# A hybrid decoder layer: load order and splits at its start, softplus steps, and one low part moved to VectorE

## The chip, the cores and the metric

The kernel runs on one core of a Trainium2 chip. The metric is the device time of one execution in microseconds (us), the median over runs. TensorE (PE) multiplies matrices into PSUM; VectorE (DVE), ScalarE (ACT) and GpSimd (POOL) do the elementwise work; SyncE (SP) issues the DMA transfers. Each engine works off its own queue in order.

## The reference

One decoder layer on 1040 tokens (16 learned meta tokens ahead of 1024), width 1024, all in float32. The part that matters here is its start:

```python
xn = rms_norm(h, mix_pre_g)                  # pre-norm
proj = xn @ w_in                             # z | x, B, C | dt | q | k | v
...
xbc = silu(causal_dwconv(xbc, conv_w, conv_b))   # 4 taps
dt = softplus(dt_raw + dt_bias)
Adt = dt * A
...                                          # SSD scan over chunks of 128, decays from cumsum(Adt)
y = rms_norm((y_diag + y_off + xs * d_skip) * silu(z), norm_g)
```

Behind it come a stick-breaking attention on q, k, v, an output projection, and a feed-forward block with a convolution of 3 taps. The change touches none of these.

## The kernel before

**Precision.** A matmul in float32 is made of three in a faster format: each operand is split into a high part (`hi`, a copy that rounds, by ScalarE) and a low part (`lo` = value minus high part, by VectorE or GpSimd), and the products hi·hi, hi·lo and lo·hi are added in PSUM. So every weight tile must be loaded (raw), split, and only then used. Names: `wr_` or `r` is a raw tile, `whi`/`wh_`/`ah` a high part, `wlo`/`wl_`/`al` a low part.

**Order.** Everything here is written inside regions of a manual schedule: within a region each engine executes its instructions in the order in which the program emits them. There are two such regions one behind the other, the *head* (lines 323 to 611) and *order* (from line 613). How instructions of the one fall among those of the other on an engine is left to the scheduler. SyncE's queue belongs to the head region too.

**The head.** It loads nine token tiles (`load_x`, tile 0 being the 16 meta tokens), the pre-norm's weights broadcast to all partitions (`gpre`, 512 KB), and weights. For tile i, `square(i)` on ScalarE sums the squares, `root(i)` makes the reciprocal root in two small steps on GpSimd (lines 169 and 170), `norm(i)` multiplies on VectorE (line 369), and `turn_x(i)` transposes on PE (line 383); ScalarE copies the high parts and two raw sums (lines 393 to 396), and VectorE subtracts for the low parts (line 402). Between them stand the products that can start early: dt (`dt_steps`, `pj_dt`), B (`pj_B`) and C (`pj_C`) of group 0, each in four parts over the tokens (`chains`, one part run at a time). `split_hi` and `split_lo` make B's and C's high part on ScalarE and low part on VectorE. At the head's end the sums of tokens that a Strassen scheme needs are split (`t1` to `t3`: line 254 on ScalarE, 255 on VectorE).

**The order region.** Column blocks of the projection are made in pairs (`Duo`): x, z, x, z, B and C, and so on. A pair takes seven products (Strassen's scheme in Winograd's form), each of 24 matmuls into one of the banks A, X or Y. Products 1 and 2 are copied out by ScalarE, the others added to an earlier result by VectorE (line 320), and a bank that goes on accumulating waits for that add. Beside the products of a pair run, in slots behind each product:

- the preparation of the next pair's weights: `split_22` (one quarter, 128x512: high part `ah` on ScalarE, line 277, low part `al` on GpSimd, line 278), `sums` (four additions of 128x512 on GpSimd, lines 285 to 288), `split_3`, `split_1`, `split_4` (whole tiles; low parts on GpSimd, line 182);
- what is left to do for the pair before (convolution taps on VectorE, lines 505 and 508; silu on ScalarE; transposes to token order);
- the steps of dt (`dt_acts`).

The first pair (`i == 0`, x) takes its products in the order 1, 5, 2, 6, 7, 3, 4. Behind product 1 it emits `d0.split_4()`, then `split_22` of the next pair (z), then slot 0, in which are taps 0 and 1 of B's convolution and dt's loads; slot 1, behind product 5, has B's taps 2 and 3. Product 7 goes on in the bank of product 6, behind its add.

dt's steps: `turn_dt` (dt to token order by small matmuls, line 649), `soft_a` and `soft_b` (softplus as a series on VectorE, with one exponential on ScalarE), three `decay` steps (each a matmul on PE, lines 682 and 683, and exponentials), the last with the stores.

Of the kernel before, what the change touches and what calls it, by code (L numbers as in the profile page):

```python
# [9 lines left out]
F32 = mybir.dt.float32  # L10
# [3 lines left out]
ALU = mybir.AluOpType  # L14
# [52 lines left out]
def tile_layer(ctx: ExitStack, tc: tile.TileContext, x, meta, rows, parts,  # L67
# [190 lines left out]
    class Duo:  # L258
# [11 lines left out]
        def split_1(self):  # L270
            self.w["a11"], self.w["a12"] = split_w(self.r[0], f"1{self.nm}")

        def split_22(self):
            h, l = (weight_rows(sa.tile([P, 5 * P], F32R, tag=f"a22{e}", name=f"a{e}{self.nm}", bufs=2), 4, OFF22)
                    for e in "hl")
            raw = self.r[1][:, HI4]
            nc.scalar.activation(h, raw, AF.Copy)
            nc.gpsimd.tensor_tensor(l, raw, h.bitcast(F32), op=ALU.subtract)
            self.w["a22"] = h, l

        def sums(self):
# [42 lines left out]
    with tc.tile_pool(name="pre", bufs=3, side="right") as pre:  # L324
# [3 lines left out]
        def load_x(i):  # L328
            xts.append(pre.tile([P, D], F32, tag="xt", name=f"xt{i}", bufs=8))
            nc.sync.dma_start(out=xts[i][:spans[i][1]], in_=meta if i == 0 else x[(i - 1) * P:i * P, :])  # L330

        def raw_of(name, src):
            raw = wp.tile([P, KB, P], F32, tag="wraw", name=f"wr_{name}")
            nc.sync.dma_start(out=raw, in_=src)
            return raw

        load_x(0)
        load_x(1)
        raws = {"B0": raw_of("B0", w_xbc[8])}
        gpre = row_bcast(pre, 0, D, "gpre")  # L340
        load_x(2)
        load_x(3)
        raw_dt = pre.tile([P, KB, 16], F32, tag="wdt", name="wr_dt", bufs=1)
        nc.sync.dma_start(out=raw_dt, in_=w_dt)
# [9 lines left out]
        def square(i):  # L354
            if i <= NT:
                nr = spans[i][1]
                junk = pre.tile([P, D], BF16, tag="junk", name=f"junk{i}", bufs=1)
                sums[i] = pre.tile([P, 1], F32, tag="ss", name=f"ss{i}")
                nc.scalar.activation(junk[:nr], xts[i][:nr], AF.Square, scale=D ** -0.5, accum_out=sums[i][:nr])
# [5 lines left out]
        def norm(i):  # L365
            if i <= NT:
                nr = spans[i][1]
                norms[i] = pre.tile([P, D], F32, tag="xn", name=f"xn{i}", bufs=2)
                nc.vector.scalar_tensor_tensor(norms[i][:nr], xts[i][:nr], roots[i][:nr], gpre[:nr],
                                               op0=ALU.mult, op1=ALU.mult)  # L370
# [3 lines left out]
        def turn_x(i):  # L374
            t0, nr = spans[i]
            tps = []
            for hf in range(2):
                tp = (psum_tp, psum_z, psum_sd)[(2 * i + hf) % 3](f"xtp{i}_{hf}")
                if (2 * i + hf) % 3:
                    tp = tp.rearrange("p (a b) -> p a b", b=P)  # L380
                for b in range(4):
                    k = 4 * hf + b
                    nc.tensor.transpose(tp[:, b, :nr], norms[i][:nr, k * P:(k + 1) * P], ident[:nr, :nr])
                tps.append(tp)
            cuts = [(t0, t0 + nr)] if t0 >= TH or t0 + nr <= TH else [(t0, TH), (TH, t0 + nr)]
            sub, copy = nc.vector.tensor_tensor, nc.scalar.activation
            for a, e in cuts:
                half = a // TH
                c = (slice(None), slice(None), slice(a - half * TH, e - half * TH))
                p0, p1 = (tp[:, :, a - t0:e - t0] for tp in tps)  # L390
                pairs = [(p0, xo[f"b1{1 + half}"]), (p1, xo[f"b2{1 + half}"])]
                for src, (h, _) in pairs:
                    copy(h[c], src, AF.Copy)
                copy((t1r, t3r)[half][c], p0, AF.Copy)
                if half == 0:
                    copy(t4r[c], p1, AF.Copy)
                for r, o in ((TH - 8, 0), (L - 8, 8)):
                    if a <= r < e:
                        for hf in range(2):
                            copy(xtail[:, 4 * hf:4 * hf + 4, o:o + 8], tps[hf][:, :, r - t0:r - t0 + 8], AF.Copy)  # L400
                for src, (h, l) in pairs:
                    sub(l[c], src, h[c].bitcast(F32), op=ALU.subtract)
                    if half and src is p0:
                        sub(t1r[c], p0, t1r[c], op=ALU.subtract)
                if half:
                    sub(t2r[c], p1, t1r[c], op=ALU.subtract)
                    late.append(lambda c=c: nc.vector.tensor_tensor(t4r[c], t4r[c], t2r[c], op=ALU.subtract))
                    sub(t3r[c], p1, t3r[c], op=ALU.subtract)
# [3 lines left out]
        def split_hi(name):  # L412
            hi = wp.tile([P, KB, P], F32R, tag="whi", name=f"wh_{name}", bufs=WB)
            lo = wp.tile([P, KB, P], F32R, tag="wlo", name=f"wl_{name}", bufs=WB)
            nc.scalar.activation(hi, raws[name], AF.Copy)
            ws[name] = hi, lo

        def split_lo(name):
            nc.vector.tensor_tensor(ws[name][1], raws[name], ws[name][0].bitcast(F32), op=ALU.subtract)
# [3 lines left out]
            root(i)  # L423
        norm(0)
        norm(1)
        split_hi("B0")
        split_lo("B0")
        square(2)
        root(2)
        norm(2)  # L430
        turn_x(0)
        square(3)
        root(3)
        norm(3)
# [190 lines left out]
    def dt_acts():  # L625
# [30 lines left out]
        def soft_a():  # L656
            dtx = box["dtx"]
            e, s, s2 = box["e"], box["s"], box["s2"] = [t3(n) for n in ("e1", "s1", "s2")]
            nc.vector.scalar_tensor_tensor(e, dtx, -1.0, dtx, op0=ALU.mult, op1=ALU.min)
            nc.scalar.activation(e, e, AF.Exp)  # L660
            nc.vector.tensor_scalar(s, e, 2.0, None, op0=ALU.add)
            nc.vector.reciprocal(s, s)
            nc.vector.tensor_tensor(s, s, e, op=ALU.mult)
            nc.vector.tensor_tensor(s2, s, s, op=ALU.mult)
# [13 lines left out]
        def decay(k):  # L678
            lhs = (tri, low, ones)[k]
            pz, adt, dst = psum_mm(f"pz{k}"), box["s2"], dtk[:, 2 + k]  # L680
            w0 = P if k == 2 else NM
            mm(pz[:w0, 0:16], lhs[:NM, :w0], adt[:NM, 0, :], start=True, stop=True)
            mm(pz[:, 16:NA], lhs, adt[:, 1:, :], start=True, stop=True)
            nc.scalar.activation(dst[:w0, 0, :], pz[:w0, 0:16], AF.Exp)
            nc.scalar.activation(dst[:, 1:, :], pz[:, 16:NA].rearrange("p (a b) -> p a b", b=16), AF.Exp)
            if k == 0:
                nc.vector.tensor_copy(dtk[:NM, 1, 0, :], pz[:NM, 0:16])
                nc.vector.tensor_copy(dtk[:, 1, 1:, :], pz[:, 16:NA].rearrange("p (a b) -> p a b", b=16))
# [15 lines left out]
        def store():  # L704
            nc.sync.dma_start(out=dtkd, in_=dtk)

        return [[loads], [turn_dt], [soft_a], [soft_b], [lambda: decay(0)], [lambda: decay(1)],
                [lambda: decay(2), store, turn_acs]]

    v_stack = ExitStack()  # L710
# [29 lines left out]
    def merged(*lists):  # L740
        return [sum(parts_, []) for parts_ in zip(*lists)]
# [5 lines left out]
    for i, q in enumerate(duos):  # L747
        n = duos[i + 1] if i + 1 < len(duos) else None
        if i + 2 < len(duos):
            duos[i + 2].load()  # L750
        for j, m in enumerate((1, 5, 2, 6, 7, 3, 4) if i == 0 else (1, 6, 5, 7, 2, 3, 4)):
            q.product(m)
            if i == 0:
                if m == 1:
                    d0.split_4()
                elif m == 6:
                    split_t(t4l.bitcast(F32), xo["t4"], nc.vector)
            if n is not None:
                if m == 1:
                    n.split_22()  # L760
                elif m == 6:
                    n.sums()
                elif m == 7:
                    n.split_3()
                elif m == 2:
                    n.split_1()
                elif m == 3:
                    n.split_4()
            elif m in (7, 2):
                v_split(1, int(m == 2))  # L770
            for act in slots[j]:
                act()
        extra = slots[7:]
        slots = q.done(q)
        for k, acts_ in enumerate(extra):
            slots[k] = acts_ + slots[k]
        if i == 1:
            slots = merged(slots, [[], dts[2], [], dts[3], [], [], []]) + [dts[4], dts[5], dts[6]]
        if i == n_early:
            t_stack.close()  # L780
            vl = v_stack.enter_context(tc.tile_pool(name="vl", bufs=1, side="left"))
            fetch_v(1, 0, vl)
        if i + 2 == len(duos):
            fetch_v(0, 0, None)
# [1711 lines left out]
```

## Time and profile before

| | |
|---|---|
| time of three runs | 1655.59 to 1659.79 us, median 1657.96 |
| the profiled execution, its time | 1657.8 us |
| its span on the core | 1655.8 us |
| granted clock of TensorE, mean of the span | 0.997 |
| instructions | 28995 |
| busy: PE, VectorE, GpSimd, ScalarE | 98%, 66%, 47%, 45% of the span |
| traffic in DRAM | 148 GB/s over the span |
| idle time of PE in the first 300 us, by the releaser | 12.1 us for the pre-norm, 2.9 us for others |

The span runs from the first to the last instruction of the execution; its time has some 2 us around it. A row of a timeline gives the start and the duration in us, the engine, the line of the kernel, the operation, out<-in with shapes, and in brackets how long the engine had stood idle before and what released it. Waits for several semaphores are put down to one of them. In the rows of the windows the busy time of PE, of its weight loads, VectorE, ScalarE and GpSimd follow one another, with the count of instructions, then the granted clock, the share of the DMA engines and GB/s.

### The profile page before, as it was taken

To read this page: it belongs to the slowest core of one execution; us is meant where nothing else is said; L and a number is where in the kernel's file an instruction comes from. 1 tells how busy PE (TensorE), PEld (TensorE's weight loads), DVE (VectorE), ACT (ScalarE), POOL (GpSimd) and SP (SyncE) were. 2 spreads that over 40 slices of the span, in tenths; PEclk is the share of its full clock that TensorE was granted. 3 is DMA by queue.
4 is the path that set the end of the run, shared out by engine and by line. 5 is a ranking of instruction groups with operands and counts; after the bars stand their busy time and mean duration, and the time that the engine had idled before them with its cause. 6 is when DMAs were issued, how large, how long until landed. Compare 5 with 4: busy or idle time off the path is not lost.

```text
span 1655.8 us, 28995 instructions
## 1 busy us (share of the span) xinstructions
PE 1626.7 (98%) x11508; PEld 1434.1 (87%) x11508; DVE 1087.5 (66%) x1248; ACT 748.1 (45%) x1100; POOL 782.1 (47%) x579
## 2 busy tenths in 40 slices
PE   7999999999999999999999999999999999999998
PEld 6999999978877888888877889999999999888886
DVE  6975744344367599999840677765666556658877
ACT  7454344332234367766741445433333333344544
POOL 2876877520457463454421113777777677200001
PEclk9999999999999999999999999999999999999999
DMA  4544335334588776545254542222333322495345
GB/s 173 185 154 133 104 121 194 135 138 145 148 236 266 212 235 207 155 123 154 60 193 151 165 161 90 96 96 96 98 107 113 108 98 83 142 332 175 96 119 180
DMA packets 164518, 247.39 MB, mean 149 GB/s; under 512 B 18487, under 2 KB 99495, under 8 KB 162702
## 3 DMA queue, kind: packets, MB, share of 16 engines
q1 hardware_dynamic: 163806, 244.48, 45.8%
q8 instruction: 91, 1.49, 0.4%
q10 hardware_dynamic: 576, 1.05, 0.2%
q14 instruction: 45, 0.37, 0.1%
HBM read 161.99 MB, written 83.46 MB: 148 GB/s over the span
## 4 chain that ended last, share of the span: by engine, by line
PE 89%; DVE 5%; issue 2%; POOL 2%; DMA 2%; ACT 1%; POOLq 0%; DVEq 0%; SPq 0%; ACTq 0%
PE fX L1900 10%; PE mo L1504 10%; PE dnA L2312 7%; PE fY L1900 7%; PE fA L1900 7%; PE dnB L2312 5%; PE av L1352 3%; PE tw L1332 3%; PE z L1308 3%; PE pj_q L218 3%; DVE kp L1314 2%; PE pj_k L218 2%; PE dXz L308 2%; PE dXqk L308 2%; PE dXx L308 2%
## 5 line engine op out<-in xcount | busy, mean ns | idle before, releaser
L1314 DVE TENSOR_TENSOR_SCAN kp<-kp,hold 128x396 f32<-128x396 f32 (+5 forms) x224 | 211.2, 1014 | 20.2 <-ACT kp L1309 18.4
L182 POOL TENSOR_TENSOR wlo<-wr,whi 128x1024 fp32r<-128x1024 f32 x43 | 99.3, 2318 | 40.8 <-ACT whi L181 40.8
L2349 POOL TENSOR_TENSOR fms<-fms 128x1 f32<-128x1 f32 x8 | 2.3, 288 | 222.0 <-DMA ar<-fda 185.9
L181 ACT ACTIVATE whi<-wr 128x1024 fp32r<-128x1024 f32 x43 | 45.7, 1063 | 112.2 <-PE fX L1900 76.2
L1972 DVE SCALAR_TENSOR_TENSOR ga<-gr,pp,ga 128x1024 f32<-128x1024 f32 x44 | 69.4, 1577 | 34.1 <-ACT ga L1965 33.3
L2234 ACT ACTIVATE dh<-ar 128x512 fp32r<-128x512 f32 x77 | 48.6, 631 | 94.1 <-PE dnB L2312 44.7
L2235 DVE TENSOR_TENSOR dl<-ar,dh 128x512 fp32r<-128x512 f32 x77 | 53.2, 691 | 47.1 <-ACT dh L2234 47.1
L1309 ACT ACTIVATE kp<-z 128x788 f32<-128x788 f32 (+4 forms) x96 | 72.7, 832 | 16.6 <-PE z L1308 12.4
L1337 ACT ACTIVATE th<-tw 128x1024 f32<-128x1024 f32 (+2 forms) x96 | 70.8, 813 | 15.6 <-PE tw L1332 15.6
L1352 PE MATMUL av<-th,v 128*64 128x128 f32 x1152 | 70.0, 275 | 2.0 <-POOL tmsa L985 0.9
L1332 PE MATMUL tw<-ident,kp 128*128 128x128 f32 x576 | 70.0, 276 | 0.8 <-ACT st L935 0.5
L1332 PEld LDWEIGHTS tw<-ident,kp 128*128 128x128 f32 x576 | 62.4, 141 | 8.0 <-issue 6.5
L1352 PEld LDWEIGHTS av<-th,v 128*64 128x64 f32 x1152 | 62.3, 137 | 8.0 <-issue 3.9
L2312 PE MATMUL dnA<-dl,dh 128*128 128x512 f32 x176 | 68.5, 389 | 0.0
L2312 PE MATMUL dnA<-dh 128*128 128x512 f32 x176 | 68.5, 389 | 0.0
L2312 PE MATMUL dnA<-dh,dl 128*128 128x512 f32 x176 | 68.5, 389 | 0.0
L1286 POOL TENSOR_SCALAR cb<-kp 128x32 f32<-128x32 f32 x64 | 42.9, 678 | 50.5 <-DVE kp L1314 46.9
L2033 POOL TENSOR_TENSOR al<-wr,ah 128x512 fp32r<-128x512 f32 x20 | 28.6, 1430 | 77.6 <-ACT ah L2032 77.5
L1308 PE MATMUL z<-k,q 64*128 64x396 f32 (+9 forms) x672 | 62.3, 329 | 1.0 <-DVE st L941 1.0
L1308 PEld LDWEIGHTS z<-k,q 64*128 64x128 f32 x672 | 53.1, 185 | 10.8 <-ACT th L1337 4.2
L2312 PE MATMUL dnB<-dh 128*128 128x512 f32 x132 | 51.3, 389 | 0.0
L2312 PE MATMUL dnB<-dh,dl 128*128 128x512 f32 x132 | 51.3, 389 | 0.0
(987 smaller groups left out, 6026.4 us busy)
## 6 DMA issues: line engine op xcount, KB each, us to landing
wr<-in_w_up SPq DMA_DIRECT2D x44, 512.0 KB
fds<-ga SPq DMA_DIRECT2D x44, 256.0 KB
b<-in_w_down SPq DMA_DIRECT2D x44, 256.0 KB
ar<-fds SPq DMA_DIRECT2D x44, 256.0 KB
fda<-ga SPq DMA_DIRECT2D x33, 256.0 KB
ar<-fda SPq DMA_DIRECT2D x33, 256.0 KB
k<-qkd SPq DMA_DIRECT2D x8, 1040.0 KB
q<-qkd SPq DMA_DIRECT2D x64, 128.0 KB
```

The source lines that it names most:

```text
L182: nc.gpsimd.tensor_tensor(l, raw, h.bitcast(F32), op=ALU.subtract)
L218: mm(acc[:, :CQ - s], a[:, k, :], b[:, k % 4, c + s:c + CQ], start=(k == 0 and j == 0), stop=(k == KB - 1 and j == 2))
L308: mm(acc[:, c, :CQ], u[:, k, :], v[:, k, c * CQ:(c + 1) * CQ], start=first and k == 0 and j == 0, stop=k == 3 and j == 2, skip_group_check ...
L1308: mm(z[:, j, a - lo:e - lo], u[h, :], r[h, a - bases[x]:e - bases[x]], start=s_ == 0, stop=s_ == 2)
L1309: nc.scalar.activation(kp[:, :, lo:top], z[:, :, :top - lo], AF.Sigmoid, scale=-QSCALE)
L1314: nc.vector.tensor_tensor_scan(part, part, hold[:, L - last + a:L - last + e][:, ::-1], 1.0 if e == last else kp[:, j, e:e + 1], op0=ALU.m ...
L1332: nc.tensor.transpose(tw[:, j, b, :], kp[:, j, c0:c0 + P], ident)
L1337: copied[0] = nc.scalar.activation(th[:, :, :nb, :], tw[:, :, :nb, :], AF.Copy, scale=-1.0, bias=1.0).ins
L1352: mm(av[halves[j], 1 - x, :], v[:, kb, halves[j]], th[:, j, b, :], start=kb == 0, stop=kb == i)
L1504: recent[0] = mm(acc, u[:, k, :], v[:, cs], start=(k == 0 and j == 0), stop=(k == 7 and j == 2))
L1900: mm(acc[:, c, :nn], u[:, k, :], v[:, k, c0:c0 + nn], start=first and k == 0 and j == 0, stop=k == 3 and j == 2, skip_group_check=not first)
L2312: mm(banks[BANK[n], t], u[:, 0, c], v[:, 1, :], start=(n in (1, 2, 5) and p == 0 and i == 0), stop=(p == NPR - 1 and i == 2), skip_group_c ...
```

## The change

It has three parts.

1. At the head, the loads of the pre-norm's weights and of token tile 2 are issued ahead of B's weights. Square, root and norm of tile 2 come ahead of B's split; its high part comes ahead of the turn of tile 0, its low part behind it.
2. dt's softplus step `soft_a` ends with the exponential; what followed there is a step of its own, `soft_m`. During the third pair `soft_a` stays behind the second product, `soft_m` comes behind the third, `soft_b` behind the fifth instead of the fourth. The decays stay where they are.
3. `split_22` takes the engine of its subtraction as an argument. For the first pair, that is for the weights of the first z pair, it is VectorE; for all others it stays GpSimd.

```diff
-        def split_22(self):
+        def split_22(self, eng=nc.gpsimd):
...
-            nc.gpsimd.tensor_tensor(l, raw, h.bitcast(F32), op=ALU.subtract)
+            eng.tensor_tensor(l, raw, h.bitcast(F32), op=ALU.subtract)
...
         load_x(0)
         load_x(1)
-        raws = {"B0": raw_of("B0", w_xbc[8])}
         gpre = row_bcast(pre, 0, D, "gpre")
         load_x(2)
+        raws = {"B0": raw_of("B0", w_xbc[8])}
         load_x(3)
...
         norm(0)
         norm(1)
-        split_hi("B0")
-        split_lo("B0")
         square(2)
         root(2)
         norm(2)
+        split_hi("B0")
         turn_x(0)
+        split_lo("B0")
         square(3)
         root(3)
         norm(3)
...
             nc.vector.scalar_tensor_tensor(e, dtx, -1.0, dtx, op0=ALU.mult, op1=ALU.min)
             nc.scalar.activation(e, e, AF.Exp)
+
+        def soft_m():
+            e, s, s2 = box["e"], box["s"], box["s2"]
             nc.vector.tensor_scalar(s, e, 2.0, None, op0=ALU.add)
...
-        return [[loads], [turn_dt], [soft_a], [soft_b], [lambda: decay(0)], [lambda: decay(1)],
+        return [[loads], [turn_dt], [soft_a], [soft_m], [soft_b], [lambda: decay(0)], [lambda: decay(1)],
                 [lambda: decay(2), store, turn_acs]]
...
                 if m == 1:
-                    n.split_22()
+                    n.split_22(nc.gpsimd if i else nc.vector)
...
         if i == 1:
-            slots = merged(slots, [[], dts[2], [], dts[3], [], [], []]) + [dts[4], dts[5], dts[6]]
+            slots = merged(slots, [[], dts[2], dts[3], [], dts[4], [], []]) + [dts[5], dts[6], dts[7]]
```

## The prediction

> **What bounds the kernel now.** I read the page first, then the waits of TensorE (PE) in the first 300 us, then the timelines of the single engines. PE fills the span, and all that the change touches lies in the first 130 us, so the question is only which waits of PE there go or come. In the waits the columns are total, number, longest.
>
> ```profile
> span 1655.8 us, 28995 instructions
> PE 89%; DVE 5%; issue 2%; POOL 2%; DMA 2%; ACT 1%; POOLq 0%; DVEq 0%; SPq 0%; ACTq 0%
> ...
> PE xtp L383 <- DVE xn L369: 12.1, 5, 10.2
> PE dXz L308 <- POOL wlo4z L182: 1.0, 1, 1.0
> ```
>
> Beside small ones of 0.6 and 0.3 us and the one at 69.23 (quoted below), these are all of PE's waits up to 300 us. PE stands until 10.2 us and in pieces until 16.8, and once at 85.5. A microsecond saved before either place moves all that follows, since PE is busy nearly without a break behind it; a microsecond that PE doesn't wait for is worth nothing. The sum is made against the profiled execution: 1657.8 us, of which 1655.8 are span. The median of the three runs, 1657.96, is 0.2 above it, less than their scatter (4.2).
>
> **Part 1, the order at the start.** Timelines, start and duration first, idle time before and its releaser in brackets:
>
> ```profile
> 7.18 1.06 ACT L415 ACTIVATE wh_B<-wr_B 128x1024 fp32r<-128x1024 f32 x1
> 10.04 1.06 ACT L359 ACTIVATE junk<-xt 128x1024 bf16<-128x1024 f32 x1 [1.80 <-DMA xt<-in_x]
> ...
> 16.61 0.62 ACT L393 ACTIVATE b21h<-xtp 128x512 fp32r<-128x512 f32 x1
> ...
> 21.60 0.38 ACT L249 ACTIVATE sq<-pj_dt 32x260 f32<-32x260 f32 x1 [0.41 <-PE pj_dt L247]
> 8.83 2.47 DVE L369 SCALAR_TENSOR_TENSOR xn<-xt,rs_pre,gpre 16x1024 f32<-16x1024 f32 x2 [6.71 <-DMA gpre<-in_rows]
> 11.23 1.20 DVE L419 TENSOR_TENSOR wl_B<-wr_B,wh_B 128x1024 fp32r<-128x1024 f32 x1
> 13.21 1.28 DVE L369 SCALAR_TENSOR_TENSOR xn<-xt,rs_pre,gpre 128x1024 f32<-128x1024 f32 x1 [0.78 <-POOL rs_pre L170]
> 15.26 1.49 DVE L369 SCALAR_TENSOR_TENSOR xn<-xt,rs_pre,gpre 128x1024 f32<-128x1024 f32 x1 [0.50 <-POOL rs_pre L170]
> ...
> 23.13 1.22 DVE L419 TENSOR_TENSOR wl_C<-wr_C,wh_C 128x1024 fp32r<-128x1024 f32 x1
> 7.22 0.23 POOL L169 TENSOR_SCALAR ms_pre<-ss 128x1 f32<-128x1 f32 x1 [2.07 <-ACT junk L359]
> 11.28 1.24 POOL L169 TENSOR_SCALAR ms_pre<-ss 128x1 f32<-128x1 f32 x1 [3.17 <-ACT junk L359]
> ...
> 13.26 1.31 POOL L169 TENSOR_SCALAR ms_pre<-ss 128x1 f32<-128x1 f32 x1
> 16.80 1.97 PE L383 MATMUL xtp<-ident,xn 128*128 128x128 f32 x8 [0.29 <-DVE xn L369]
> 18.42 1.22 PE L247 MATMUL pj_dt<-b11h,wh_dt 128*32 128x260 f32 x4
> ...
> 25.39 0.28 PE L218 MATMUL pj_C<-b11h,wl_C 128*128 128x260 f32 x1
> ```
>
> The transfers land one behind the other: B's weights by 7.2 (ScalarE starts on them then, unwaited), the norm's weights at 8.8, token tile 2 at 10.0. All three are 512 KB, so in the new order I put the same three landings: norm's weights about 7.4, tile 2 about 8.7, B's weights about 10.0 (an estimate; the total ahead of 10.0 is unchanged). On SyncE's queue B's load is passed by these two and passes none. Behind them the load of x's first weights waits for B's low part, which frees its buffer (12.4, now about 13.5); what is queued behind it has time, its weights being read past 40.
>
> ScalarE: square 2 moves from 10.04 to 8.7, and B's high part takes its place at 10.04 with the same 1.06. So ScalarE reaches tile 0's copies at 11.1 as before, and as it has hardly an idle moment from 10.04 until its wait before 21.60 it gains next to nothing. VectorE: norms 0 and 1 at 7.4 to 9.9. GpSimd: root 2 at 9.9 and not at 12.5. Its first step takes 0.23 alone, but 1.24 and 1.31 where B's low part (11.23) or norm 2 (13.21) runs on VectorE: it waits until that ends. Norm 2 then runs at 10.8 to 12.0, B's low part at 12.2 to 13.5, root 3 behind that at 13.5 to 14.3, norm 3 at 14.3 to 15.6. Before, norm 3 ended at 16.75; 1.2 earlier. PE's transposes of tile 3 and the first product of dt (18.42) follow it directly: 17.2. The next to be late is ScalarE's copy of tile 2 (ends 17.2, in time), then C's low part, which stays at 24.3 less about 0.2, while PE wants it at 25.4 less 1.2: just in time. I take **-1.1**; bounds 0 (ScalarE, which gains nothing, takes over) and -1.6 (the wait for root 3 vanishes too). B's low part, now 1.2 to 2 later, is covered: PE's first use is past 20. From norm 6 on the VectorE chain follows PE, so the gain is carried to 42 us and beyond.
>
> **Part 2, the softplus.** It adds and drops no instruction.
>
> ```profile
> 115.79 1.17 DVE L661 TENSOR_SCALAR s<-e 128x144 f32<-128x144 f32 x1 [2.75 <-ACT e L660]
> ...
> 128.30 0.31 DVE L675 SCALAR_TENSOR_TENSOR s<-dtk,expa 128x144 f32<-128x144 f32 x1
> 129.34 0.14 PE pz L682 x2
> ```
>
> The last row is of the chain of waits. VectorE stands 2.75 us for ScalarE's exponential, with the add of the product that ended meanwhile queued behind it. The change lets this add go first; soft_b comes a slot later, but the product of the slot between is copied by ScalarE, so on VectorE it stays behind the same add. It ends some 0.6 earlier than 128.6, and its reader on PE comes at 129.34: PE doesn't wait before or after. **0**; the cover is 0.7 us, and if soft_b came later by more, PE would wait by the rest.
>
> **Part 3, z's low part by VectorE.** Here a wait is added, and this decides.
>
> ```profile
> 58.91 1.95 ACT L254 ACTIVATE t3h<-t3r 128x2080 fp32r<-128x2080 f32 x1 [3.35 <-DVE t2l L255]
> ...
> 62.46 0.62 ACT L277 ACTIVATE ahz<-wrz 128x512 fp32r<-128x512 f32 x1
> ...
> 58.80 0.81 DVE L505 TENSOR_SCALAR cdB<-craw_B,pp 128x1040 f32<-128x1040 f32 x1
> 59.65 1.30 DVE L508 SCALAR_TENSOR_TENSOR cdB<-craw_B,pp,cdB 128x1040 f32<-128x1040 f32 x1
> ...
> 60.95 2.31 DVE L255 TENSOR_TENSOR t3l<-t3r,t3h 128x2080 fp32r<-128x2080 f32 x1
> ...
> 63.79 4.77 DVE L508 SCALAR_TENSOR_TENSOR cdB<-craw_B,pp,cdB 128x1040 f32<-128x1040 f32 x2
> 68.49 0.69 DVE L320 TENSOR_TENSOR craw_x<-dXx,craw_x 128x520 f32<-128x520 f32 x1
> ...
> 75.81 2.21 DVE L508 SCALAR_TENSOR_TENSOR cdC<-craw_C,pp,cdC 128x1040 f32<-128x1040 f32 x1
> 62.65 2.67 POOL L182 TENSOR_TENSOR wlo4x<-s24x,whi4x 128x1024 fp32r<-128x1024 f32 x1 [5.95 <-ACT whi4x L181]
> 65.27 2.19 POOL L278 TENSOR_TENSOR alz<-wrz,ahz 128x512 fp32r<-128x512 f32 x1
> ...
> 75.18 1.75 POOL L287 TENSOR_TENSOR s24z<-wrz,wrz 128x512 f32<-128x512 f32 x1
> 77.00 2.17 POOL L288 TENSOR_TENSOR s24z<-wrz,s24z 128x512 f32<-128x512 f32 x1
> 69.23 0.39 PE L308 MATMUL dXx<-t3h,whi3x 128*128 128x260 f32 x1 [0.96 <-DVE craw_x L320]
> 81.95 2.09 PE L649 MATMUL tpd<-fold,sq 32*16 32x16 f32 x18
> 83.97 0.39 PE L308 MATMUL dXz<-t2h,whi4z 128*128 128x260 f32 x1
> 85.52 0.58 PE L308 MATMUL dXz<-t2h,wlo4z 128*128 128x260 f32 x1 [1.05 <-POOL wlo4z L182]
> 89.93 2.87 PE dYz L308 x24
> 86.00:87.00 1.00, 1.00 (x7) 1.00 (x7) 0.96 (x2) 0.03 (x1) 0.89 (x1) 0.50 0.99 406
> ```
>
> What it removes: GpSimd works without a break from 62.65 until wlo4z, for which PE waits at 85.5; al of z is 2.19 of that (half of it waiting). With it gone wlo4z comes about 2 us earlier, before PE wants it at 84.4. The wait is dear, since the granted clock falls to 0.50 there (last row, of the windows: the third number from the end). In the chain of waits the next product follows at 89.93, so this one, begun at 83.97, took 6.0 us; a neighbour takes 2.87 and some 0.2 to start. So **-2.9**: 1.2 of standing and 1.7 of half clock. The matmul at 83.97, ahead of the wait, still took 0.39 as the one at 69.23 did, the first behind it 0.58: the clock fell within the wait. If it falls without it too, only 1.2 goes.
>
> [...]
>
> What it adds: al of z is emitted behind the first product, ahead of B's convolution taps 0 and 1, and VectorE keeps the emitted order within the region. Its input ah is ready at 63.1. Before, the two taps ran at 58.80 to 60.95, while VectorE had nothing else to do and GpSimd stood. Now they queue behind al. Only t3l, of the region before, can go ahead (input ready at 60.9): 60.95 to 63.2. Queued behind al: both taps, the add of product 5, taps 2 and 3, and the add at 68.49, for which PE's next product (69.23) waits.
>
> From 63.2 GpSimd is never free, and the two engines take turns: at 75.18 to 79.2 each instruction ends where the other's real run begins (76.9, 78.0, 79.2), 1.2 for a tap or a half tile on GpSimd, 2.1 for a whole tile. The add, which reads PSUM, takes 0.7 regardless. I walk it through: GpSimd's wlo4x to 65.3; al to 65.9 (half of wl_B's 1.20); tap 0 to 66.7; wlo1z to 68.8; tap 1 to 70.0; a half tile to 71.2, beside it the add of product 5; tap 2 to 72.4; a half tile to 73.6; tap 3 to 74.8; the add to 75.4. So 75.4 against 69.2: **+6.2**. The bounds: no turn lost, +0.7 (63.2 + 0.6 + 0.8 + 1.3 + 0.1 + 0.7 + 2.6 + 0.7 = 70.0); one more whole tile, +8.3. I take the walk, as its rule is read from the nearest rows.
>
> PE then stands from 68.3 to 75.4, long enough to lose the clock: another **+1.6**, the half-clock part of the place above (0 if it held). GpSimd has time enough for wlo4z in this case too, so the -2.9 stays.
>
> **Sum:** 1657.8 - 1.1 + 0 + 6.2 + 1.6 - 2.9 = **1661.6**. Its own bounds, with the terms' ends not all on one side: 1657.5 to 1664.
>
> **Rivals.** *VectorE keeps pace* (the turns aren't lost, no clock drop): 1657.8 - 1.1 + 0.7 - 2.9 = 1654.5. For it: the lower bound; against it: every tap beside GpSimd in the rows. Chance 0.14. *ScalarE takes the first product's copy, whi4x and ah ahead of t3h*: ScalarE stands 3.35 us before t3h; if these three (some 2 us) fell there, ah would be ready 3 us sooner, both taps would run before t3l, and the add, some 2 late, wouldn't cost the clock: 1657.8 - 1.1 + 2 - 2.9 = 1655.8, up to 1657.5. Against it: the order of before has t3h first. 0.10. *Slower*: VectorE takes al ahead of t3l; t3l's 2.2 then come behind 63.1 with one more turn of about 1.2: +3 on the forecast, 1664.6. It decides if the order puts al ahead of t3l, though t3l is ready 2 us sooner. 0.06. *The start gives nothing*: B's weights land a microsecond later than tile 2 did, ScalarE's chain and PE's start move back: 1662.7. 0.08. The forecast keeps 0.62.
>
> **How the numbers follow.** What a measurement can tell from no change is about 0.3%, 5 us: faster is below 1653.0, slower above 1662.9. Around each case I leave some 2 us for the terms' bounds and the runs. Slower: 0.15 of the forecast's 0.62, nearly all of the third rival, half of the fourth: 0.24. Faster: a third of the first rival and little else: 0.06. The range reaches from 1654.0 (the first rival) to 1664.0, leaving out half of the third rival and the tails.
>
> **What would show it.** Right: the low part of z's first weights on VectorE right behind t3l, taps 0 and 1 after 65, PE's wait for the add near 69 grown to some 7 us with the granted clock 0.5 after it, and no wait for wlo4z; norm 3 ending near 15.6 and dt's first product near 17.2. Wrong: taps that still run before 61, or that take 1.3 beside GpSimd; a PE wait near 69 under 2 us; tile 2 landing no earlier than 10.

## The result and the profile after

| | before | after |
|---|---|---|
| time, median us (lowest to highest, runs) | 1656.90 (1655.59 to 1659.79, 6) | 1662.92 (1661.23 to 1664.01, 6) |
| ratio to before, 95% interval | 1 | 1.0029 [1.0019, 1.0039] |
| profiled execution, us; its span | 1657.8; 1655.8 | 1661.68; 1659.9 |

The changed kernel is slower, by 0.19 to 0.39%. By the bound of 0.3% that the prediction took, 0.29% is on the edge between no change and slower; the six runs of each kernel do not overlap. One run of a kernel below, p1_only, took 2288.94 us at a granted clock of 0.655 and is not in its ratio.

The waits of PE in the changed kernel's first 300 us (total, number, longest):

```profile
PE xtp L383 <- DVE xn L369: 10.7, 4, 8.5
PE dXx L308 <- DVE craw_x L320: 7.4, 1, 7.4
PE pj_C L218 <- DVE wl_C L419: 0.7, 1, 0.7
PE pz L685 <- DVE s L678: 0.4, 1, 0.4
```

The reader sees three changes: the first wait is 1.4 us shorter, a wait of 7.4 us for the second add stands where 1.0 stood, and the wait for wlo4z is gone. Two small waits are new, 0.7 us for C's low part and 0.4 for the softplus. The timelines of the changed kernel around that add (start, duration, engine; in brackets idle time and its releaser):

```profile
59.04 2.33 DVE L255 TENSOR_TENSOR t3l<-t3r,t3h 128x2080 fp32r<-128x2080 f32 x1 [2.01 <-ACT t3h L254]
61.28 2.68 DVE L278 TENSOR_TENSOR alz<-wrz,ahz 128x512 fp32r<-128x512 f32 x1
63.88 0.81 DVE L505 TENSOR_SCALAR cdB<-craw_B,pp 128x1040 f32<-128x1040 f32 x1
64.73 3.21 DVE L508 SCALAR_TENSOR_TENSOR cdB<-craw_B,pp,cdB 128x1040 f32<-128x1040 f32 x1
67.86 1.23 DVE L636 TENSOR_TENSOR fold<-ident 32x16 f32<-32x16 f32 x1
69.02 0.68 DVE L320 TENSOR_TENSOR craw_x<-dYx,craw_x 128x520 f32<-128x520 f32 x1
69.63 3.50 DVE L508 SCALAR_TENSOR_TENSOR cdB<-craw_B,pp,cdB 128x1040 f32<-128x1040 f32 x2
73.06 0.69 DVE L320 TENSOR_TENSOR craw_x<-dXx,craw_x 128x520 f32<-128x520 f32 x1
60.80 2.61 POOL L182 TENSOR_TENSOR wlo4x<-s24x,whi4x 128x1024 fp32r<-128x1024 f32 x1 [5.95 <-ACT whi4x L181]
...
64.65 2.19 POOL L182 TENSOR_TENSOR wlo1z<-wrz,whi1z 128x1024 fp32r<-128x1024 f32 x1 [0.60 <-ACT whi1z L181]
66.80 2.27 POOL L285 TENSOR_TENSOR wrz<-wrz 128x512 f32<-128x512 f32 x1
69.14 2.89 POOL L286 TENSOR_TENSOR wrz<-wrz,wrz 128x512 f32<-128x512 f32 x1
```

VectorE has hardly a gap from 59.04 to 73.75. The taps, which before began at 58.80, begin at 63.88, behind alz. What meets GpSimd there is long: alz 2.68, tap 1 3.21, where before it took 1.30 with GpSimd standing still. Even `fold`, an addition of 32x16 numbers, takes 1.23 us; before, where it ran ahead of GpSimd's work, it took 0.16. And the windows of the same kernel, 2 us each (width, busy us and instructions of PE, PEld, DVE, ACT, POOL, then granted clock, DMA share, GB/s):

```profile
70.00:72.00 2.00, 0.00 (x0) 0.00 (x0) 1.97 (x2) 0.00 (x0) 2.00 (x2) 0.50 0.00 0
72.00:74.00 2.00, 0.20 (x1) 0.20 (x2) 1.74 (x2) 0.83 (x1) 2.00 (x2) 0.50 0.00 0
74.00:76.00 2.00, 2.00 (x10) 2.00 (x11) 0.00 (x0) 2.00 (x2) 1.56 (x2) 0.50 0.00 0
76.00:78.00 2.00, 2.00 (x11) 2.00 (x11) 1.91 (x1) 0.06 (x1) 0.00 (x0) 0.50 0.56 113
78.00:80.00 2.00, 2.00 (x16) 1.99 (x15) 1.27 (x3) 0.91 (x1) 0.00 (x0) 0.83 0.96 355
80.00:82.00 2.00, 2.00 (x19) 2.00 (x18) 1.96 (x2) 0.30 (x2) 1.77 (x1) 1.00 0.20 73
```

The clock falls within PE's wait (by 69 us; PE stands from 66.4 to 73.8) and stays 0.50 for five microseconds behind it: 10 and 11 matmuls in 2 us, 19 once it is back.

### The profile page after: what moved, and what is told of

Same layout as the page of the kernel before. It is cut to its first block, busy times and chain, and to the rows that moved or that the text cites. A ratio compares the mean times of both kernels' runs of the same rounds, so it can differ in the third digit from the quotient of the medians.

```text
span 1659.9 us, 28993 instructions
## 1 busy us (share of the span) xinstructions
PE 1624.6 (98%) x11508; PEld 1431.8 (86%) x11508; DVE 1092.4 (66%) x1249; ACT 748.1 (45%) x1100; POOL 777.3 (47%) x578
## 4 chain that ended last, share of the span: by engine, by line
PE 60%; DVE 2%; issue 1%; POOL 1%; ACT 0%; DMA 0%; SPq 0%; POOLq 0%; DVEq 0%; ACTq 0%
PE fX L1903 10%; PE mo L1507 10%; PE dnA L2315 7%; PE fY L1903 7%; PE fA L1903 7%; PE dnB L2315 5%; PE av L1355 3%; PE tw L1335 3%; PE z L1311 2%; DVE kp L1317 2%; PE g0a L1917 1%; PE x2tp L1781 0%; PE pj_k L218 0%; PE g0d L1917 0%; PE g0c L1917 0%
## 5 line engine op out<-in xcount | busy, mean ns | idle before, releaser
L1317 DVE TENSOR_TENSOR_SCAN kp<-kp,hold 128x396 f32<-128x396 f32 (+5 forms) x224 | 211.4, 1014 | 20.1 <-ACT kp L1312 18.3
```

What stands on the lines that cost most here:

```text
L1317: nc.vector.tensor_tensor_scan(part, part, hold[:, L - last + a:L - last + e][:, ::-1], 1.0 if e == last else kp[:, j, e:e + 1], op0=ALU.m ...
```

## The experiments

Ten kernels were run in three sets, each set beside the kernel before on the same chip; the changed kernel's own comparison is a fourth, so differences to its median reach across sets (the medians of before lie within 0.5 us). "dAx to add" is the time from the first product's first matmul on the x pair to the first matmul behind the second add: whatever happened at the start is taken out of it. "Add to dYz" is the time from there to z's third product. Both are from the one profiled execution of each kernel.

| kernel | time us | ratio, 95% interval | dt's first product at | dAx to add | wait for the add | add to dYz | wait for wlo4z | half clock, 60 to 100 us |
|---|---|---|---|---|---|---|---|---|
| before | 1656.4 to 1656.9 | 1 | 18.4 | 14.1 | 1.0 | 20.5 | 1.0 | near 85 to 89 |
| after | 1662.92 | 1.0029 [1.0019, 1.0039] | 16.4 | 20.5 | 7.4 | 19.9 | none | 68 to 79 |
| p1_only | 1656.32 | 0.9994 [0.9985, 1.0004] | 17.0 | 14.1 | 1.0 | 20.4 | 1.0 | near 83 to 87 |
| p12 | 1656.61 | 0.9999 [0.9990, 1.0007] | 17.1 | 14.1 | 1.0 | 20.5 | 1.1 | near 84 to 87 |
| p3_only | 1662.65 | 1.0034 [1.0021, 1.0047] | 18.5 | 20.5 | 7.4 | 20.4 | none | 71 to 81 |
| p13 | 1662.48 | 1.0032 [1.0020, 1.0043] | 17.0 | 20.5 | 7.4 | 20.3 | none | near 69 to 80 |
| taps_first | 1656.55 | 1.0002 [0.9993, 1.0010] | 16.3 | 16.4 | 3.3 | 19.2 | none | 85 to 88 |
| busy_pe | 1661.58 | 1.0028 [1.0017, 1.0039] | 16.8 | 20.6 | filled but for 1.5 | 17.7 | none | none |
| no_reads | 1655.11 | 0.9994 [0.9985, 1.0003] | 17.1 | 14.7 | 2.1 | 19.2 | none | 70 to 73 |
| p12_memset | 1655.63 | 0.9993 [0.9984, 1.0001] | 17.0 | 14.2 | 1.0 | 20.3 | 1.0 | 83 to 87 |
| alz_late | 1654.99 | 0.9989 [0.9980, 0.9998] | 17.0 | 15.3 | 2.2 | 19.2 | none | 69 to 73 |
| alz_late_spread | 1655.64 | 0.9991 [0.9982, 1.0000] | 17.1 | 15.3 | 2.2 | 18.3 | 0.7 | none |

### Which part costs the time

**p1_only**: part 1 alone. Against the changed kernel:

```diff
-        return [[loads], [turn_dt], [soft_a], [soft_m], [soft_b], ...
+        return [[loads], [turn_dt], [soft_a], [soft_b], ...
...
-                    n.split_22(nc.gpsimd if i else nc.vector)
+                    n.split_22()
```

> Part 1 alone (loads and splits at the start), the rest as before. My theory: TensorE's first product of dt starts near 16.4 us as in the changed kernel, the wait for z's last low part and its half clock stay, so about 1.9 us faster than before. Rival (the start is bound by ScalarE, and what is gained there is lost by 45 us): no change, and a dt product near 18.4 or a wait that comes instead.

**p3_only**: part 3 alone, with the loads, the splits and the softplus as in the kernel before.

```diff
         load_x(1)
+        raws = {"B0": raw_of("B0", w_xbc[8])}
         gpre = row_bcast(pre, 0, D, "gpre")
         load_x(2)
-        raws = {"B0": raw_of("B0", w_xbc[8])}
...
-        return [[loads], [turn_dt], [soft_a], [soft_m], [soft_b], ...
+        return [[loads], [turn_dt], [soft_a], [soft_b], ...
```

> Part 3 alone (one low part of z by VectorE), the rest as before. My theory: the wait for the add grows to about 7.4 us, half a clock behind it, the wait for z's last low part goes: 5 to 6.5 us slower than before. Rival (the loss comes from the new order at the start, and part 3 only removes a wait): 2 to 3 us faster than before.

**p12**: parts 1 and 2.

```diff
...
-                    n.split_22(nc.gpsimd if i else nc.vector)
+                    n.split_22()
```

> Parts 1 and 2 without part 3. My theory: part 3 is the whole loss, so this is faster than both: about 1.9 us under before, 6 to 8 us under the changed kernel; part 2 gives nothing. Rival (softplus in two parts costs its share of the loss): no better than before.

**p13**: parts 1 and 3.

```diff
...
-        return [[loads], [turn_dt], [soft_a], [soft_m], [soft_b], ...
+        return [[loads], [turn_dt], [soft_a], [soft_b], ...
```

> Parts 1 and 3 without part 2. My theory: the changed kernel less its 0.4 us wait of the first decay on softplus, so 0 to 0.5 us under the changed kernel and 4 to 6 above before. Rival (part 2 lets the adds go earlier and so helps): slower than the changed kernel by a microsecond or more.

The two kernels without part 3 are within 0.1% of before, the two with it 0.32 and 0.34% above. One part makes the whole loss, and the table says where: "dAx to add" is 20.5 us in the three kernels that have part 3 as the change has it (p3_only, p13, after), and 14.1 in those without (p1_only, p12, before). p13 and after do not differ beyond their intervals, nor do p1_only and p12: part 2 is worth nothing that these runs can tell. p3_only and p13 came out as expected. Neither p1_only nor p12 shows the 1.9 us expected of part 1, and dt's first product starts at 17.0 and 17.1 there, not at 16.4.

In the profile part 1's gain is there at the start: in p1_only dt's first product begins at 17.0 (18.4 before), and the lead is 1.8 us at V's first product (335.5 against 337.3). Then comes a wait of PE that before doesn't have. It stands in the first fence, from p1_only's waits; the other two are the loads of V's weights in SyncE's queue, from the timelines of before and of p1_only:

```profile
PE vtail L848 <- DMA vq<-in_w_v: 0.8, 2, 0.5
```
```profile
344.74 1.41 SPq L721 DMA_DIRECT2D vq<-in_w_v  x3
```
```profile
343.74 1.92 SPq L721 DMA_DIRECT2D vq<-in_w_v  x4
```

PE comes 1.8 us earlier to V's products, but V's weights are asked for only 1.0 us earlier. At the first product of q the lead is 0.7 (419.8 against 420.5). The rest of this profile's lead goes in a stretch of half clock of 6.8 us at 592 us that before's profile doesn't have. In alz_late's profile, with the same start, the wait is 0.2 and the lead still 1.6 at the first product of q (418.9). So the loads are one place where part of the lead can go; they do not always take it. The intervals of p1_only (2.5 us under to 0.7 above) and p12 (1.7 under to 1.2 above) leave open what is left at the end, if anything.

### What in part 3 costs it

**no_reads** leaves work out: GpSimd writes zeros where it would read and compute, and so reads nothing from 55.0 to 73.4 us of its profile.

```diff
-        nc.gpsimd.tensor_tensor(l, raw, h.bitcast(F32), op=ALU.subtract)
+        if nm in ("4x00", "1z00"):
+            nc.gpsimd.memset(l.bitcast(F32), 0.0)
+        else:
+            nc.gpsimd.tensor_tensor(l, raw, h.bitcast(F32), op=ALU.subtract)
...
+            if self.nm == "z00":
+                for t in (r2[:, HI4], r2[:, LO4], s24[:, LO4], s24[:, HI4]):
+                    nc.gpsimd.memset(t, 0.0)
+                return
```

> Leaves out part of the computation: the low parts of x's fourth and z's first weights and z's weight sums are zeros, written by GpSimd's memset, so that GpSimd reads nothing from 57 to 77 us. Theory (VectorE's operations with two inputs in SBUF and GpSimd's that read SBUF run in turns, each ending with or behind the other): alz takes about 0.6 us rather than 2.68, taps 1 to 3 take 1.30 each rather than 1.7 to 3.2, the second add ends at 67 to 69 us rather than 73.75, PE's wait for it falls from 7.4 to 1 to 2.5 us, the clock stays whole, and the time is 5 to 8 us under the changed kernel's. Rival (VectorE's operations are long for themselves, or wait for data): alz stays over 2 us, the second add comes after 72 us, and the time falls by under 2 us.

Timelines of no_reads (its line numbers are 3 to 7 higher):

```profile
59.20 2.33 DVE L258 TENSOR_TENSOR t3l<-t3r,t3h 128x2080 fp32r<-128x2080 f32 x1 [2.01 <-ACT t3h L257]
61.44 0.68 DVE L281 TENSOR_TENSOR alz<-wrz,ahz 128x512 fp32r<-128x512 f32 x1
62.05 0.82 DVE L512 TENSOR_SCALAR cdB<-craw_B,pp 128x1040 f32<-128x1040 f32 x1
62.90 1.30 DVE L515 SCALAR_TENSOR_TENSOR cdB<-craw_B,pp,cdB 128x1040 f32<-128x1040 f32 x1
...
64.81 2.62 DVE L515 SCALAR_TENSOR_TENSOR cdB<-craw_B,pp,cdB 128x1040 f32<-128x1040 f32 x2
67.35 0.69 DVE L327 TENSOR_TENSOR craw_x<-dXx,craw_x 128x520 f32<-128x520 f32 x1
63.19 0.96 POOL L183 MEMSET wlo1z<- 128x1024 f32 x1 [6.65 <-PE dAx L315]
64.09 0.99 POOL L290 MEMSET wrz<- 128x512 f32 x2
```

VectorE's order is the changed kernel's, instruction for instruction, and alz stands at the head of the taps. But alz takes 0.68 and not 2.68, tap 1 1.30 and not 3.21, taps 2 and 3 2.62 and not 3.50; the second add ends at 68.0 and not 73.75. GpSimd stands still beside alz, but its memsets run beside taps 1 to 3, as the last two rows show, and take no turns. So it is GpSimd's subtractions and additions that stretch VectorE's operations here, and not its memsets (tap 1 takes 3.21 beside a subtraction and an addition, 1.30 beside memsets), and the 5.7 us of the add are turns. Whether their reading or their arithmetic does it, this run doesn't separate. An operation with one input is not always spared: in before, tap 0 of C's convolution (74.60, line 505) takes 1.18 us beside one of z's sums and a first tap of x's (84.44, the same line) 1.58 beside z's last low part, where tap 0 of B's takes 0.81. The wait of 2.1 is within the expected 1 to 2.5; the expected whole clock is a miss (0.50 from 69.7 to 73.1), and the time, 7.8 us under the changed kernel's, is right.

**taps_first** keeps alz on VectorE and puts B's taps 0 and 1 ahead of it.

```diff
                 elif m == 6:
                     split_t(t4l.bitcast(F32), xo["t4"], nc.vector)
+            if i == 0 and m == 1:
+                for act in slots[0][:2]:
+                    act()
+                slots[0] = slots[0][2:]
             if n is not None:
```

> The changed kernel with B's taps 0 and 1 issued on VectorE ahead of z's alz on the first pair. Theory (the loss is VectorE's order: alz at the head of the taps makes every tap meet a GpSimd operation, and they take turns): taps 0 and 1 run at 0.81 and 1.30 us right behind t2l, near 57 to 59 us, alz still takes its turn with wlo4x and ends near 64.0, the second add ends near 70 to 71 us rather than at 73.75, PE's wait for it falls from 7.4 to 3.5 to 4.5 us, with at most one stretch of half clock, and the time is 2 to 5 us under that of the changed kernel, 1658 to 1661 us. Rival (alz costs only its own 2.7 us wherever it stands): the wait stays at 6 to 7.4 and the time at 1662 to 1663.

Timelines of taps_first:

```profile
56.83 0.81 DVE L505 TENSOR_SCALAR cdB<-craw_B,pp 128x1040 f32<-128x1040 f32 x1
57.68 1.30 DVE L508 SCALAR_TENSOR_TENSOR cdB<-craw_B,pp,cdB 128x1040 f32<-128x1040 f32 x1
58.93 2.33 DVE L255 TENSOR_TENSOR t3l<-t3r,t3h 128x2080 fp32r<-128x2080 f32 x1
61.17 2.68 DVE L278 TENSOR_TENSOR alz<-wrz,ahz 128x512 fp32r<-128x512 f32 x1
...
64.47 4.42 DVE L508 SCALAR_TENSOR_TENSOR cdB<-craw_B,pp,cdB 128x1040 f32<-128x1040 f32 x2
68.81 0.69 DVE L320 TENSOR_TENSOR craw_x<-dXx,craw_x 128x520 f32<-128x520 f32 x1
```

alz starts and ends within 0.2 us of where it stood, and takes the same 2.68. Only the two taps have moved, to the time before t3l when GpSimd stands still, and the add ends at 69.5 and not at 73.75. PE's wait of 3.3 is just under the expected 3.5 to 4.5. The time is that of the kernel before, 6.4 us under the changed kernel's median, where 2 to 5 were expected; the stage accounts for 4.75 of it (4.13 of "dAx to add", 0.62 of "add to dYz"), the rest can't be placed. So of the 6.4 us that part 3 adds up to the add, 4.1 are the two places that the taps lost; 2.3 stay, with alz's turn on VectorE still in the way. Up to dYz 1.0 us stays (35.6 against 34.6 before), with a stretch of half clock in each.

**busy_pe** gives PE something to do in the wait.

```diff
                 elif m == 6:
+                    idle = psum_mm("idle")
+                    for k in range(50):
+                        mm(idle[:, :CQ], d0.w["s2"][0][:, k % 4, :], xo["t2"][0][:, k % 4, :CQ], start=k == 0, stop=k == 49)
                     split_t(t4l.bitcast(F32), xo["t4"], nc.vector)
```

> The changed kernel with 50 matmuls of 128x260 behind product 6 of the first pair, into a bank that nothing reads, so that PE has work in its wait for the second add. Theory (the half clock behind the add is the answer to PE's idle time, and costs some 1.6 us beside the wait): the add ends at 73 to 74 us as before the edit, the granted clock stays 1.00 from 70 to 78 us, dYx starts on the same time, and z's first products are 1.5 to 2 us earlier than in the changed kernel unless PE then waits for wlo4z, which took 2.9 us in the kernel before: so the time is 1.6 less to 1.3 us more than the changed kernel's. Rival (the half clock has another cause): the clock falls at 70 us all the same, and z's first products start where they did.

PE in busy_pe, a window and a row of its timeline:

```profile
74.00:76.00 2.00, 2.00 (x17) 2.00 (x17) 0.00 (x0) 2.00 (x2) 1.73 (x2) 1.00 0.00 0
```
```profile
73.96 0.39 PE L308 MATMUL dXx<-t3h,whi3x 128*128 128x260 f32 x1 [1.50 <-DVE craw_x L320]
```

The add comes as late as ever, but the clock stays 1.00, 17 matmuls in a window that had 10, and "add to dYz" is 17.7 against 19.9 in the changed kernel: in these two profiles the half clock behind the wait costs 2.1 us. In the time this can't be told: 1661.58, within the expected bounds, but with the changed kernel's interval. The profiled execution, the only one whose stage is seen, had a mean clock of 0.999 and was the fastest of the seven (1657.88); the six others have 0.996 to 0.998, so they lost clock somewhere. Where, stays open.

### Whether alz on VectorE can pay

**p12_memset** leaves alz on GpSimd and takes the memset of dtk, 0.70 us, off GpSimd's chain.

```diff
+    nc.gpsimd.memset(dtk, 0.0)
...
         def loads():
...
-            nc.gpsimd.memset(dtk, 0.0)
```

> Parts 1 and 2 of the change without part 3, and the memset of dtk (0.70 us of GpSimd ahead of z's low parts) moved to the kernel's beginning. Theory (PE's wait for wlo4z near 84 us, 1.0 us and a stretch of half clock, is GpSimd's chain being late): wlo4z ends 0.5 to 0.7 us earlier against PE, the wait falls to 0.3 to 0.6 us; if the clock then holds, the time is 1.5 to 2.5 us under that of parts 1 and 2 alone, else 0.5 to 0.7 us. Rival (the chain is set by ScalarE's whi4z or by the turns, not by GpSimd's order): the wait stays at 1.0 us and the time is the same within 0.5 us.

A miss. The wait for wlo4z is 1.0 as before, although the memset is gone from the chain: wlo1z, which now starts earlier, meets VectorE otherwise and takes 3.20 us, against 2.56 in p12. What the order gave, the turns took back, as the rival had it; 1655.63 can't be told from before.

**alz_late** leaves alz on VectorE and issues it behind the second add, where VectorE stood for 2.4 us.

```diff
-            eng.tensor_tensor(l, raw, h.bitcast(F32), op=ALU.subtract)
+            self.low22 = lambda: eng.tensor_tensor(l, raw, h.bitcast(F32), op=ALU.subtract)
+            if eng is nc.gpsimd:
+                self.low22()
...
                 elif m == 6:
+                    n.low22()
                     split_t(t4l.bitcast(F32), xo["t4"], nc.vector)
```

> The changed kernel with alz still on VectorE, but issued behind the second add (ahead of t4l) on the first pair, where VectorE stood idle for 2.4 us in every run so far. Theory (part 3's fault is the place in VectorE's order and not the engine): taps run as in the kernel before, the second add ends at 67 to 68.5 us, PE waits 1.0 to 1.5 us for it, GpSimd is rid of 2.2 us, so that wlo4z ends near 81 to 82.5 and PE's wait for it (1.0 with alz on GpSimd) is gone; dYz starts at 86.5 to 88 us (88.3 with parts 1 and 2, 93.7 in the changed kernel) and the time is 1654.5 to 1656.5 us, 6 to 8 us under the changed kernel's. Rival (an operation of VectorE beside GpSimd's low parts costs its turns wherever it stands): alz takes over 2.5 us behind the add, t4l is late for PE by over 1 us, GpSimd's chain is no shorter, and the time is 1657 us or more.

Timelines of alz_late:

```profile
56.96 0.81 DVE L507 TENSOR_SCALAR cdB<-craw_B,pp 128x1040 f32<-128x1040 f32 x1
...
61.95 5.98 DVE L510 SCALAR_TENSOR_TENSOR cdB<-craw_B,pp,cdB 128x1040 f32<-128x1040 f32 x2
67.85 0.69 DVE L322 TENSOR_TENSOR craw_x<-dXx,craw_x 128x520 f32<-128x520 f32 x1
68.46 0.68 DVE L278 TENSOR_TENSOR alz<-wrz,ahz 128x512 fp32r<-128x512 f32 x1
69.22 1.28 POOL L287 TENSOR_TENSOR wrz<-wrz 128x512 f32<-128x512 f32 x1 [2.38 <-DVE alz L278]
79.99 3.21 POOL L182 TENSOR_TENSOR wlo4z<-s24z,whi4z 128x1024 fp32r<-128x1024 f32 x1
```

alz now takes 0.68, its length when nothing contends, since GpSimd is standing: the sum at 69.22 writes into the raw tile that alz reads, so it waits 2.38 us for alz. That gives back nearly all that GpSimd was spared: wlo4z ends at 83.2 and not by 82.5, 29.9 us behind dAx, where p12 has 30.4. Taps 2 and 3 beside z's first low part lose a turn more (5.98 us, against 4.77 before and 4.42 in taps_first), so PE waits 2.2 for the add and not 1.5, and the clock fell behind that wait in this execution. dYz starts at 87.8, as expected, and the wait for wlo4z is gone, but only because PE came later. The time, 1654.99, is the one of the study whose ratio's interval lies wholly under 1: 0.02 to 0.20% faster, and 7.9 us under the changed kernel's median. As one of ten intervals, and under the bound of 0.3%, that is weak. The stage itself (dAx to dYz, 34.5 us) is only 0.1 us shorter than before's (34.6); the lead of the start, 1.6 at q's first product in this profile, does more. That alz on VectorE pays for itself is not shown.

**alz_late_spread** also deals out dt's small products.

```diff
-        def turn_dt():
-            tpd, dtb = psum_mm("tpd"), box["dtb"]
-            for i in range(NT + 1):
+        def turn(i0, i1):
+            tpd = box["tpd"] = psum_mm("tpd") if i0 == 0 else box["tpd"]
+            for i in range(i0, i1):
...
+        def turn_dt():
+            turn(6, NT + 1)
...
-        return [[loads], [turn_dt], ...
+        return [[loads], [lambda: turn(0, 3)], [lambda: turn(3, 6)], [turn_dt], ...
...
```

> As alz_late, and the small products that turn dt (18 records of 32x16, 2.09 us on end) issued in three groups behind three of z's products rather than all behind the first. Theory (the half clock from about 84.5 to 88 us, which came with no wait of PE in the run with B's taps first, is the answer to 2.1 us of small products on end): the granted clock stays 1.00 from 80 to 92 us, z's first products are 1.5 to 1.9 us earlier than in alz_late if the clock fell there, and the time is 1 to 2 us less. Rival (the clock falls by a phase that this does not touch): a stretch of half clock of 3 to 4 us stands between 80 and 95 us here too, or the time is the same within 0.7 us.

Inconclusive. The clock is 1.00 from 60 to 100 us, but alz_late itself kept it from 80 on, with all the small products on end, so this tells nothing of them. With the same wait for the add (2.19 us, 2.17 in alz_late) it kept the clock that alz_late lost there. The median is no lower.

## Why the prediction was right, and where not

It was made against the profile, 1661.6 against 1661.68 there; the median is 1662.92. By its steps, with "dYz" as the place where the change's stretch ends: forecast -1.1 + 6.2 + 1.6 - 2.9 = +3.8 us, measured 89.8 to 93.7, +3.9.

The mechanism is the one forecast; that the sum fits to 0.1 us is luck. From dAx to dYz the change costs 5.75 us (40.4 against 34.6), where 6.2 + 1.6 - 2.9 makes 4.9, and the lead at dAx is 1.85, where 1.1 was forecast: two errors that cancel. Behind dYz they part again. At q's first product the profiles are 5.0 us apart (425.5 against 420.5), and only a stretch of half clock of 3.4 us near 468, which before's profile has and after's has not, brings their ends back to 3.9. The medians are 6.0 us apart, close to what part 3 costs alone (6.2 in p3_only).

- **The add, +6.2: right, with its mechanism.** "dAx to add" went from 14.1 to 20.5, +6.4. The walk through the turns holds at the operations that it names: with the start's lead of 1.85 us added back, alz ends at 65.8 (walk 65.9), tap 0 at 66.5 (66.7), tap 1 at 69.8 (70.0), tap 3 at 75.0 (74.8), the add at 75.6 (75.4). What the walk doesn't have is `fold`: it stands between tap 1 and the add of product 5 and took the turn there (to 70.9) that the walk gives to a half tile ahead of tap 2. no_reads takes the mechanism away whole, taps_first for the two taps that it moves.
- **The half clock behind the add, +1.6: right in kind, a little short.** It measured 2.1 (19.9 less 17.7 of busy_pe); p3_only and p13 have 2.6. The prediction took its size from the place near 86 us (where it has 1.7 itself); there the half clock lasted 3.4 us, here 10.2, and 4.9 of them fell on matmuls. That a stand from 68.3 to 75.4 is "long enough to lose the clock" was the author's estimate; no run shows how long is enough. The clock fell within the waits of 7.4 us and, in before, within the one of 1.0 for wlo4z; it fell behind those of 2.1 (no_reads) and 2.2 (alz_late), and it held in those of 1.0 for the add (before), 2.2 (alz_late_spread) and 3.3 (taps_first).
- **wlo4z, -2.9: right.** Without wait and half clock the stretch from the add to dYz takes 17.7, before it took 20.5: 2.8. But the part that is half clock is not bound to the wait: taps_first had no wait there and lost the clock all the same, which is the prediction's "if it falls without it too, only 1.2 goes". In the six other profiles without the wait (after, p3_only, p13, busy_pe, no_reads, alz_late) it didn't fall at that place, though the same 18 small products of dt ran there; so whether these have a part in the fall stays open.
- **Part 1, -1.1: too small at its own place, too large at the end.** The order came out as drawn: norm's weights, tile 2, B's high part at 9.81, norm 3 ending at 15.5, where 15.6 was forecast. The lead at dAx is 1.85, since PE also ran faster at the start (the eight transposes ahead of dt's first product took 1.09 us, 1.97 before; below); in the nine other profiles with this start it lies between 0.3 and 2.0. C's low part, "just in time" in the prediction, was 0.7 us late here and 0.6 in taps_first, the two in which dt's first product starts by 16.4; in the others it was in time. But at the end p1_only's ratio gives 1.0 us, with an interval from 2.5 under before to 0.7 above, and p12's gives 0.2. The step that the runs don't bear out is "so the gain is carried to 42 us and beyond", as far as "beyond" means the end; how much of the gain arrives there stays open.
- **Part 2, 0: right to 0.4 us.** The standing for the exponential fell as foreseen, from 2.75 us to 1.18. But soft_b didn't end earlier against PE; in after and alz_late_spread PE waits 0.4 for it (pz), in the other profiles with part 2 it doesn't. Two rows of after's timelines show where the saving went:

```profile
122.94 2.24 DVE L667 TENSOR_TENSOR s<-s 128x144 f32<-128x144 f32 x1
122.82 2.19 POOL L182 TENSOR_TENSOR wlo3z<-wrz,whi3z 128x1024 fp32r<-128x1024 f32 x1
```

  An operation that took 0.31 before met GpSimd's low part and ended just behind it: one more turn lost.
- **The rivals.** "VectorE keeps pace" fell with the taps' 3.21; "ScalarE takes the copies first" and "al ahead of t3l" with the order of the rows, t3l at 59.04 and alz behind it; "the start gives nothing" with dt's product at 16.4 in the profile, though in the time it isn't excluded.

## What to carry to other kernels

Before an operation is moved to an engine that looks free, look at what it will push behind the moment when the neighbour starts its own subtractions and additions: a tap of 1.3 us took 3.2 there, an addition of 32x16 numbers 1.23 instead of 0.16, and the same move with two taps put ahead of it cost 1.0 us of its stage and nothing that the time can tell. A low part that is needed last is better put behind the operation that the matmuls wait for (15.3 us from dAx to the add in alz_late, 20.5 in after); but what it reads may be what the other engine writes next, which then waits (GpSimd 2.38 us for alz in alz_late). A gain at the head can be lost again at the loads of a later stage, as part of it was in p1_only's profile (0.8 us of waits for V's weights).

## What the runs showed of the hardware beyond that

**In these profiles the length of PE's wait does not tell whether the clock falls.** Every stretch at 0.50 that ends within a profile lasts 3.4 us or two or three times that (6.8 at 592 us in p1_only, 10.2 in after). taps_first stood 3.29 us for the add at full clock and then lost it from 84.9 to 88.3 with no wait at all, in the midst of 128x260 matmuls, 0.5 us behind dt's small products; alz_late lost it behind a wait of 2.2 us, alz_late_spread kept it behind the same wait. Windows of taps_first, columns as above:

```profile
66.00:68.00 2.00, 0.25 (x3) 0.04 (x1) 2.00 (x1) 0.00 (x0) 2.00 (x2) 1.00 1.03 397
85.00:86.00 1.00, 1.00 (x7) 1.00 (x6) 1.00 (x3) 1.00 (x3) 0.00 (x0) 0.50 0.00 0
88.00:89.00 1.00, 1.00 (x9) 1.00 (x9) 0.00 (x0) 0.00 (x0) 0.92 (x2) 0.86 0.74 287
```

The time scatters with the mean clock: the 29 runs of before in the second set go from 1653.34 at a mean clock of 0.999 to 1659.82 at 0.995; over the 29 the correlation of the two is -0.70.

**PE ran at different speeds on the same code at the start.** alz_late and alz_late_spread have one head. The first matmul of B in each, and its duration:

```profile
19.55 0.28 PE L218 MATMUL pj_B<-b11h,wh_B 128*128 128x260 f32 x1
```
```profile
20.74 0.42 PE L218 MATMUL pj_B<-b11h,wh_B 128*128 128x260 f32 x1
```

In the one it takes 0.28, in the other the first three take 0.42 each, which is what such a matmul takes at a granted clock of 0.50 (before, 85.9 to 88.7 us). By dAx the difference is 1.6 us (53.27 against 54.86); the profile's clock column shows 1.00 in both. Part 1 moves the start by about as much as this varies.
